# Hybrid GLA / RWKV-7 encoder block on one core: FFN rows, residuals and merged branches transposed by VectorE and through DRAM, and new operands used by two products at once

## The chip, the cores and the metric

The kernel runs on 1 core of a Trainium2 chip. Its time is the device time of one execution in microseconds (us). The time before is the median of 3 runs, and one more execution was profiled.

## The reference, cut to what matters

One layer of a streaming encoder on 256 frames of 2048 channels, all in float32. It has an FFN at half weight, a mixer with two branches, a second FFN at half weight and a final normalization.

```python
x = x + 0.5 * swiglu(rmsnorm(x, ffn1_norm), ffn1_wg, ffn1_wu, ffn1_wd)   # D_FF = 5632
h = rmsnorm(x, mix_norm)
p = h @ w_in                       # GLA heads | RWKV-7 heads (token shift) | two merge gates
o_gla = gla_branch(...)            # chunks of 64 frames, 4 heads
o_rw  = rwkv7_branch(...)          # delta-rule state, 16 heads of 64
gates = sigmoid(gate_p + gate_b)
merged = gates[..., :2048] * (o_gla @ w_branch[:1024]) + gates[..., 2048:] * (o_rw @ w_branch[1024:])
x = x + merged @ w_out
x = x + 0.5 * swiglu(rmsnorm(x, ffn2_norm), ffn2_wg, ffn2_wu, ffn2_wd)
out = rmsnorm(x, final_norm)

def swiglu(h, wg, wu, wd):
    return (silu(h @ wg) * (h @ wu)) @ wd
```

## The kernel before, in words

**Products.** Frames lie on 128 partitions, in NT = 2 row tiles. A product of activations and weights takes the activations transposed (channels on partitions) as the operand that TensorE loads, and a piece of the weights, 128 channels by NB = 512 columns, as the operand that streams. Both are split into a high and a low float32r part, and each K slice of 128 channels takes three matmuls per row tile: high times high, high times low, low times high. They write a PSUM tile `pm`, 128 rows by 512 columns, of which there are four. `linear` makes one block of 512 columns for both row tiles, over nk K slices; a block of 16 K slices is 96 matmuls.

**Weights.** `wload` issues on SyncE's queue one load of 1 MB for four K slices (`raw`, three buffers). For each half of it, a weight tile of two K slices, ScalarE casts it to `hi` (line 225) and VectorE subtracts that from `raw` to give `lo` (line 226). `hi` and `lo` have three buffers each. So a weight tile is one cast, one subtraction, and 12 matmuls, and the cast of a tile waits for the matmuls of the tile three before it.

**Who sets the order.** TensorE's instructions stay in the order in which the program is written (`mm`, `tr`). ScalarE's, VectorE's and the queues' are ordered when the kernel is built by a scheduler with a timeline of its own; weight casts and subtractions have a higher priority there. Work beside the products is written as generators: `later` puts one on a list with a due time, and `linear` calls `tick` after each K slice, which steps those that are due by a clock that counts 1.28 per K slice of full width. A `yield n` puts the next step off by n. An operand that isn't there yet is asked for through a function (`of`, `Normed.__call__`), which calls `drain` until it is. On each engine instructions run in order, and one that waits holds up those behind it.

**FFN.** D_FF is 11 blocks of 512 columns, taken in groups of 4, 4 and 3. For each block `linear` makes `pg` (with wg) and `pu` (with wu), 192 matmuls together. ScalarE writes silu(pg) into `h` and VectorE multiplies it with `pu`, one row tile at a time (lines 371 and 372). The generator `hidden` then brings the two row tiles of `h` into the layout with channels on partitions: `transposed` makes four TensorE transposes (128x128, line 117) into one PSUM tile `ps` per row tile, a set, and `split` casts that (ScalarE, line 288) and subtracts (VectorE, line 289) into the halves of `hid`. The down projection of the group is four `linear`s over 16 or 12 K slices of `hid`, and VectorE adds each to the residual x (line 392).

**Normalization.** `Normed` holds the transposed residual `xh`, `xl`, scaled by the norm's gain. The row scale 1/rms comes later, at the evacuation of each product. For each block of 512 channels `block` makes two sets of four TensorE transposes and, per K slice, a ScalarE activation (line 324) and a VectorE scalar_tensor_tensor (line 325); `stats` squares and sums on ScalarE (line 306). The first normalization reads the input, the second the residual after FFN 1, the third the residual after the mixer.

**Mixer.** The first product after the second normalization is the low-rank one (464 columns), then GLA's keys and query. The recurrence of RWKV-7 runs beside the products of the mixer; there VectorE already makes 32x32 block transposes (line 846), and POOL issues small loads (`uv`, `wg`) and writes gates to DRAM and reads them back (`md`). At the end `merge(j)` makes a block of 512 merged columns in `sg` and `mg`, and `split_up` transposes it as in the FFN. Four `linear`s over 16 K slices of these give the output projection; the residual is read back from DRAM into x2.

Of the kernel before, what the change touches and what calls it, by code (L numbers as in the profile page):

```python
# [71 lines left out]
def block_kernel(ctx, tc, A, out, dbg=None):  # L72
# [214 lines left out]
    def split(hi, lo, src):  # L287
        nc.scalar.copy(hi, src)
        nc.vector.tensor_sub(lo, src, hi.bitcast(F32))

    class Normed:
# [3 lines left out]
        def __init__(self, x, g0, first=False):  # L295
            self.x, self.g0, self.done, self.first = x, g0, 0, first
# [16 lines left out]

        def block(self, c):
            x, xh, xl = self.x, self.xh, self.xl
            for kt in range(4 * c, 4 * c + 4, 2):
# [10 lines left out]
                if kt == 0 and self.first:  # L327
                    warm_up(2)
# [3 lines left out]
        def __call__(self, kt, t):  # L332
            drain(lambda: self.done > kt // 2 / 2)
# [20 lines left out]
    def ffn(pool, x, xT, wg, wu, wd, then, by_rows=None):  # L354


        for b0, nb in ((0, 4), (4, 4), (8, 3)):
            hid = []

            def hidden(hs):  # L360
                hi, lo = mk(pool, [P, 4, SEQ], "hid", F32R, 12), mk(pool, [P, 4, SEQ], "hid", F32R, 12)
                yield from transposed(hs, hi, lo)
                hid.append((hi, lo))

            for b in range(b0, b0 + nb):
                pg = linear(xT, 16, cols(wg, b * NB))
                pu = linear(xT, 16, cols(wu, b * NB))
# [8 lines left out]
            for c in range(D // NB):  # L376
                w = cols(wd[b0 * NB:(b0 + nb) * NB], c * NB)
# [11 lines left out]
                pd = linear(xhl, 4 * nb, w)  # L389
# [7 lines left out]
    with phase("f1") as f1:  # L397
# [13 lines left out]
        n1 = Normed(x, R_F1, True)  # L411
# [4 lines left out]
        def to_mixer(c):  # L416
            if not n2:
                n2.append(Normed(x, R_MIX))
            later(n2[0].block(c), 1.5)
# [17 lines left out]
        lora_ps = linear(xT, 16, lora_cols, 464)  # L437
# [163 lines left out]
    later(gla_keys(rowscaled(linear(xT, 16, cols(w_in, K_OFF)))))  # L601
    later(chan_major([gq], rowscaled(linear(xT, 16, cols(w_in, Q_OFF))), 128 ** -0.5))
# [373 lines left out]
    mt = mixer.enter_context(phase("mt"))  # L976
    merged = []

    def merge(j, ps):
# [17 lines left out]
        later(split_up(), 1.5)  # L997
# [3 lines left out]
    xp = ctx.enter_context(tc.tile_pool(name="xp", bufs=1, side="right", reuse_waits="tile"))  # L1001
# [3 lines left out]
    n3 = None  # L1005
    for c in range(D // NB):
        ps = linear(xm, 16, cols(A["w_out"][0], c * NB))
# [3 lines left out]
        n3 = n3 or Normed(x, R_F2)  # L1011
        later(n3.block(c), 1.5)
# [45 lines left out]
```

## Time and profile before

| | |
|---|---|
| time | 2326.47 us, median of 3 runs (2326.31 to 2327.11) |
| the profiled execution | 2327.71 us, of it 2325.9 us span |
| TensorE busy | 2294.5 us, 99% |
| VectorE busy | 1283.8 us, 55% |
| ScalarE busy | 1025.8 us, 44% |
| POOL busy | 68.9 us, 3% |
| TensorE clock granted | 0.992 of full in the mean |
| SyncE's DMA queue (weights) | 52.9% of 16 engines' span |
| all DMA | 423.91 MB, mean 182 GB/s |

The span runs from the first to the last instruction of the profile. A busy share is the share of the span in which the engine ran at least one instruction; matmuls are pipelined, so TensorE's says little of its pace. Weight loads of TensorE run beside its matmuls and are counted apart. Idle time of an engine is put down to what ended it. The chain of waits is followed back from the last instruction, at each step to what released it.

### The profile page before, as it was taken

What the parts mean: (1) busy time and instruction counts of PE and PEld (TensorE: products, weight loads), DVE (VectorE), ACT (ScalarE), POOL (GpSimd) and SP (SyncE); (2) the same over time, 40 slices, a digit from 0 to 9 for tenths busy, and PEclk for the clock granted to TensorE, in tenths of its full rate; (3) what the DMA queues carried; (4) which work ended last, traced back from release to release, by engine and by line L of the source; (5) the groups of instructions that cost most, each with busy time, mean ns of one, the idle gap of its engine ahead of it and who ended that gap; (6) DMA issues with size and microseconds to landing.
All of it is one profiled execution on the core that took longest, in us unless ns stands there. A gap on an engine that the chain in (4) does not pass through costs nothing.

```text
span 2325.9 us, 29306 instructions
## 1 busy us (share of the span) xinstructions
PE 2294.5 (99%) x12123; PEld 1880.6 (81%) x12123; DVE 1283.8 (55%) x1435; ACT 1025.8 (44%) x1218; POOL 68.9 (3%) x119
## 2 busy tenths in 40 slices
PE   9999999999999999999999999999999999999998
PEld 7888888888888887877778778888888888888886
DVE  5445544554555545576677746655545544554555
ACT  5443344434445554454344334454443344434443
POOL 1000000000000001010101100000000000000000
PEclk9999999999999999999999999999999999999999
DMA  7555555556556554554334436656565656555553
GB/s 253 191 183 198 191 189 191 189 193 195 198 181 204 190 181 138 189 181 132 124 127 153 128 129 240 217 185 194 182 194 186 199 184 197 185 195 191 189 187 139
DMA packets 213157, 423.91 MB, mean 182 GB/s; under 512 B 10562, under 2 KB 14896, under 8 KB 212640
## 3 DMA queue, kind: packets, MB, share of 16 engines
q1 hardware_dynamic: 207072, 404.12, 52.9%
q0 software_dynamic: 5488, 17.12, 2.2%
q8 instruction: 95, 1.56, 0.3%
q10 hardware_dynamic: 464, 0.79, 0.1%
q14 instruction: 38, 0.31, 0.0%
HBM read 412.57 MB, written 7.34 MB: 181 GB/s over the span
## 4 chain that ended last, share of the span: by engine, by line
PE 94%; DVE 2%; ACT 2%; issue 1%; DMA 1%; POOL 0%; SPq 0%; DVEq 0%; ACTq 0%; POOLq 0%
PE pm L114 87%; PE ps L114 5%; PE ps L117 2%; DVE lo L226 1%; ACT hi L225 0%; DVE rn L710 0%; POOL uv L762 0%; DMA uv<-rv 0%; ACT L711 0%; DMA raw<-in_ffn_wd_dram 0%; DVE bk L752 0%; ACT L708 0%; DMA raw<-in_ffn_wg_dram 0%; ACT pt L704 0%; ACT at L706 0%
## 5 line engine op out<-in xcount | busy, mean ns | idle before, releaser
L226 DVE TENSOR_TENSOR lo<-raw,hi 128x1024 fp32r<-128x1024 f32 (+2 forms) x763 | 926.1, 1214 | 957.5 <-ACT hi L225 956.8
L225 ACT CAST hi<-raw 128x1024 fp32r<-128x1024 f32 (+2 forms) x763 | 796.8, 1045 | 1141.4 <-PE pm L114 1123.9
L114 PE MATMUL pm<-hi,xh 128*128 128x512 f32 (+1 forms) x2080 | 827.9, 398 | 0.3 <-ACT xh L324 0.3
L114 PE MATMUL pm<-lo,xh 128*128 128x512 f32 (+1 forms) x2080 | 813.6, 391 | 4.6 <-DVE lo L226 4.6
L114 PE MATMUL pm<-hi,xl 128*128 128x512 f32 (+1 forms) x2080 | 813.0, 391 | 0.0
L114 PEld LDWEIGHTS pm<-hi,xh 128*128 128x128 f32 x2080 | 392.6, 189 | 89.7 <-issue 7.7
L114 PEld LDWEIGHTS pm<-lo,xh 128*128 128x128 f32 x2080 | 393.0, 189 | 82.5 <-DVE lo L226 5.5
L114 PEld LDWEIGHTS pm<-hi,xl 128*128 128x128 f32 x2080 | 392.4, 189 | 82.7
L114 PE MATMUL pm<-hi,hid 128*128 128x512 f32 x1384 | 432.2, 391 | 0.0
L114 PEld LDWEIGHTS pm<-hi,hid 128*128 128x128 f32 x1384 | 259.9, 188 | 53.5
L114 PE MATMUL pm<-lo,hid 128*128 128x512 f32 x692 | 269.6, 390 | 1.6 <-DVE lo L226 1.6
L114 PEld LDWEIGHTS pm<-lo,hid 128*128 128x128 f32 x692 | 130.0, 188 | 28.4 <-DVE lo L226 2.0
L114 PE MATMUL pm<-hi,ot 128*128 128x512 f32 x256 | 86.9, 407 | 0.0
L114 PE MATMUL pm<-hi,mt 128*128 128x512 f32 x256 | 81.2, 393 | 0.0
L114 PEld LDWEIGHTS pm<-hi,ot 128*128 128x128 f32 x256 | 49.2, 192 | 11.3 <-issue 0.3
L114 PEld LDWEIGHTS pm<-hi,mt 128*128 128x128 f32 x256 | 48.1, 188 | 9.8
L114 PE MATMUL pm<-lo,ot 128*128 128x512 f32 x128 | 51.0, 399 | 0.0
L114 PE MATMUL pm<-lo,mt 128*128 128x512 f32 x128 | 49.9, 389 | 0.0
L371 ACT ACTIVATE h<-pm,rinv 128x512 f32<-128x512 f32 x44 | 30.2, 686 | 19.9 <-PE pm L114 19.9
L117 PEld LDWEIGHTS ps<-cst,h 128*128 128x128 f32 (+2 forms) x234 | 29.1, 140 | 7.5
L117 PE MATMUL ps<-cst,h 128*128 128x128 f32 (+2 forms) x234 | 34.9, 272 | 0.0
L324 ACT ACTIVATE xh<-ps,vec 128x256 fp32r<-128x256 f32 x48 | 22.5, 471 | 23.3 <-DVE xl L325 15.9
(242 smaller groups left out, 1064.2 us busy)
## 6 DMA issues: line engine op xcount, KB each, us to landing
raw<-in_ffn_wu_dram SPq DMA_DIRECT2D x88, 1024.0 KB, 5.2
raw<-in_ffn_wd_dram SPq DMA_DIRECT2D x88, 1024.0 KB, 5.0
raw<-in_ffn_wg_dram SPq DMA_DIRECT2D x85, 1024.0 KB, 5.2
raw<-in_w_in_dram SPq DMA_DIRECT2D x80, 1024.0 KB, 5.1
raw<-in_w_branch_dram SPq DMA_DIRECT2D x16, 1024.0 KB, 5.0
raw<-in_w_out_dram SPq DMA_DIRECT2D x16, 1024.0 KB, 5.1
raw<-in_w_in_dram SPq DMA_DIRECT2D x4, 896.0 KB, 5.7
raw<-in_ffn_wg_dram SPq DMA_DIRECT2D x12, 256.0 KB, 4.2
```

The lines of the kernel that those rows point to most:

```text
L114: tc.keep_in_program_order(nc.tensor.matmul(*args, **kw))
L117: tc.keep_in_program_order(nc.tensor.transpose(*args))
L225: nc.scalar.copy(hi[:, k0:k1, 0:width], src)
L226: nc.vector.tensor_sub(lo[:, k0:k1, 0:width], src, hi.bitcast(F32)[:, k0:k1, 0:width])
L324: nc.scalar.activation(xh[:, kt + j, :], ps[:, j, :], AF.Copy, scale=g)
L371: nc.scalar.activation(s, pg[t], AF.Silu, scale=xT.rinv[:, t:t + 1])
```

## The change

Three things are changed.

First, `turn` takes the place of TensorE's transposes for the FFN rows (`turned` in `hidden`), for the residuals of the second and third normalization (`turned_block`) and for the merged branches (`split_up`). VectorE transposes each 128x512 row tile in 32x32 blocks into `blocks` (one buffer). A DMA that POOL issues writes `blocks` to DRAM (`aside`, 0.5 MB, two buffers), and four DMAs that POOL issues, one per group of 32 channels, read it back into `turned` (two buffers), which then holds channels on partitions. ScalarE's cast and VectorE's subtraction read `turned`, in SBUF, in the place of `ps`, in PSUM. The first normalization, GLA's outputs and the small transposes of the recurrence stay with TensorE.

Second, `two_linears` makes two products that use the same operand: the K slices of the first, all but the last group of four; then the same of the second; then the last group of the first, then of the second. It is used for the first gate and up block of each FFN, for the low-rank and key product, for the first two blocks of each down projection, and for the first two of the output projection.

Third, small things: the pool of x2 opens before the merge, since the merge now keeps its tiles there; the warm-up matmuls are tied to the first block of `block` alone; the query product is written ahead of the keys' evacuation.

```diff
+    def two_linears(xhl, nk, w0, w1, width0=NB):
+        last = nk // 4 - 1
+        pss = [linear(xhl, nk, w, n, kgs=range(last)) for w, n in ((w0, width0), (w1, NB))]
+        return [linear(xhl, nk, w, n, ps, [last]) for (w, n), ps in zip(((w0, width0), (w1, NB)), pss)]
...
+    def turn(pool, srcs):
+        blocks = mk(pool, [P, NT, 4, P], "blocks", F32, 1)
+        for t, src in enumerate(srcs):
+            nc.vector.transpose(blocks[:, t].rearrange("p b (k j) -> p b k j", k=4),
+                                src.rearrange("p (k b j) -> p b k j", k=4, b=4))
+        aside = dram.tile([P, NT, 4, P], F32, tag="aside", name=nm("aside"), bufs=2)
+        nc.gpsimd.dma_start(aside, blocks)
+        res = mk(pool, [P, NT * 4, 4, 32], "turned", F32, 2)
+        for b in range(4):
+            nc.gpsimd.dma_start(
+                res[32 * b:32 * b + 32].rearrange("i (t g) k j -> i t g (k j)", t=NT),
+                aside[:, :, b].rearrange("(g i) t n -> i t g n", g=4))
+        return res
...
+        def turned_block(self, c):
+            x, xh, xl = self.x, self.xh, self.xl
+            res = turn(self.pool, [x[:, t, c * NB:(c + 1) * NB] for t in range(NT)])
+            self.stats(c)
+            for k in range(4):
+                if k % 2 == 0:
+                    yield 1.0 if k else 4.0
+                kt = 4 * c + k
+                g = col(self.g0 + kt)
+                nc.scalar.activation(by32(xh[:, kt, :]), res[:, :, k, :], AF.Copy, scale=g)
+                nc.vector.scalar_tensor_tensor(
+                    by32(xl[:, kt, :]), res[:, :, k, :], g, by32(xh.bitcast(F32)[:, kt, :]), ALU.mult, ALU.subtract)
+                self.done += 0.25
...
+    def turned(pool, srcs, hi, lo):
+        res = turn(pool, srcs)
+        for t in range(NT):
+            yield 1.0 if t else 4.0
+            ts = slice(t * P, (t + 1) * P)
+            h4, l4 = (a[:, :, ts].rearrange("p k (g j) -> p k g j", j=32) for a in (hi, lo))
+            split(h4, l4, res[:, 4 * t:4 * t + 4].rearrange("p g k j -> p k g j"))
...
             def hidden(hs):
...
-                yield from transposed(hs, hi, lo)
+                yield from turned(pool, hs, hi, lo)
...
-                pg = linear(xT, 16, cols(wg, b * NB))
-                pu = linear(xT, 16, cols(wu, b * NB))
+                if b == 0:
+                    pg, pu = two_linears(xT, 16, cols(wg, 0), cols(wu, 0))
+                else:
+                    pg, pu = linear(xT, 16, cols(wg, b * NB)), linear(xT, 16, cols(wu, b * NB))
...
+            pds = two_linears(xhl, 4 * nb, *ws[0:2])
...
-                pd = linear(xhl, 4 * nb, w)
+                pd = pds[c] if c < 2 else linear(xhl, 4 * nb, w)
...
-            later(n2[0].block(c), 1.5)
+            later(n2[0].turned_block(c))
...
-        lora_ps = linear(xT, 16, lora_cols, 464)
+        lora_ps, key_ps = two_linears(xT, 16, lora_cols, cols(w_in, K_OFF), 464)
...
-            yield from transposed([s[:, t, :] for t in range(NT)], hi, lo)
+            yield from turned(xp, [s[:, t, :] for t in range(NT)], hi, lo)
...
+    pos = two_linears(xm, 16, *wos[0:2])
...
-        n3 = n3 or Normed(x, R_F2)
-        later(n3.block(c), 1.5)
+        n3 = n3 or Normed(x, R_F2, xp)
+        later(n3.turned_block(c))
```

The order of the instructions moves at the places where a transposed block is taken into the two halves. First ScalarE in the FFN, from the third weight tile before the end of the second block's products on. `hi` is a weight tile, made from `raw`; `hid` is the high half of the transposed block, made from the PSUM tile `ps`. Before:

```order
L225 CAST hi_841<-raw_839 128x1024
L225 CAST hi_845<-raw_839 128x1024
L225 CAST hi_891<-raw_889 128x1024
L225 CAST hi_895<-raw_889 128x1024
L288 CAST hid_855<-ps_863 128x4x128
L225 CAST hi_925<-raw_923 128x1024
L288 CAST hid_855<-ps_882 128x4x128
L225 CAST hi_929<-raw_923 128x1024
L225 CAST hi_959<-raw_957 128x1024
L225 CAST hi_963<-raw_957 128x1024
L225 CAST hi_995<-raw_993 128x1024
```

and after, with `turned` in the place of `ps`:

```order
L225 CAST hi_841<-raw_839 128x1024
L225 CAST hi_845<-raw_839 128x1024
L225 CAST hi_889<-raw_887 128x1024
L225 CAST hi_893<-raw_887 128x1024
L225 CAST hi_925<-raw_923 128x1024
L225 CAST hi_929<-raw_923 128x1024
L225 CAST hi_959<-raw_957 128x1024
L225 CAST hi_963<-raw_957 128x1024
L294 CAST hid_855<-turned_862 128x4x128 x2
L225 CAST hi_995<-raw_993 128x1024
```

The two casts of the block stood behind the second and the third weight tile of the next block (`raw_889`, `raw_923`); they now stand together behind three more tiles than the second of them did, ahead of the tile `hi_995`.

VectorE at the same place, from the last product of the rows on (`h`, line 372 before and 423 after). `lo` is the other half of a weight tile. Before:

```order
L372 SCALAR_TENSOR_TENSOR h_126_831<-pm_693,rinv_105,h_126_831 128x512
L372 SCALAR_TENSOR_TENSOR h_127_834<-pm_694,rinv_105,h_127_834 128x512
L226 TENSOR_TENSOR lo_892<-raw_889,hi_891 128x1024
L226 TENSOR_TENSOR lo_896<-raw_889,hi_895 128x1024
L289 TENSOR_TENSOR hid_856<-ps_863,hid_855 128x4x128
L226 TENSOR_TENSOR lo_926<-raw_923,hi_925 128x1024
L289 TENSOR_TENSOR hid_856<-ps_882,hid_855 128x4x128
```

and after, where `blocks` is the tile of 32x32 blocks that goes to DRAM:

```order
L423 SCALAR_TENSOR_TENSOR h_127_831<-pm_693,rinv_105,h_127_831 128x512
L423 SCALAR_TENSOR_TENSOR h_128_834<-pm_694,rinv_105,h_128_834 128x512
L303 STREAM_TRANSPOSE blocks_857<-h_127_831 128x512
L226 TENSOR_TENSOR lo_890<-raw_887,hi_889 128x1024
L303 STREAM_TRANSPOSE blocks_857<-h_128_834 128x512
L226 TENSOR_TENSOR lo_894<-raw_887,hi_893 128x1024
L226 TENSOR_TENSOR lo_926<-raw_923,hi_925 128x1024
L226 TENSOR_TENSOR lo_930<-raw_923,hi_929 128x1024
L226 TENSOR_TENSOR lo_960<-raw_957,hi_959 128x1024
L226 TENSOR_TENSOR lo_964<-raw_957,hi_963 128x1024
L295 TENSOR_TENSOR hid_856<-turned_862,hid_855 128x4x128 x2
```

Two block transposes have come in, with a weight subtraction between them, and the block's own subtractions stand behind six weight subtractions where they stood behind two and three.

Last ScalarE at the first residual block of the second normalization, in the down projection that ends FFN 1. Line 306 before and 332 after is the squaring for the row statistics; `xh` is the high half of the transposed residual. Before:

```order
L225 CAST hi_4825<-raw_4823 128x1024
L306 ACTIVATE h_788_4819,part_4761<-x_87 128x512
L306 ACTIVATE h_789_4821,part_4761<-x_87 128x512
L225 CAST hi_4829<-raw_4823 128x1024
L324 ACTIVATE xh_4763<-ps_4795,vec 128x256 x2
L225 CAST hi_4859<-raw_4857 128x1024
L324 ACTIVATE xh_4763<-ps_4810,vec 128x256 x2
```

and after:

```order
L225 CAST hi_4875<-raw_4873 128x1024
L332 ACTIVATE h_817_4899,part_4865<-x_87 128x512
L332 ACTIVATE h_818_4901,part_4865<-x_87 128x512
L225 CAST hi_4879<-raw_4873 128x1024
L225 CAST hi_4945<-raw_4943 128x1024
L332 ACTIVATE h_822_4913,part_4865<-x_87 128x512
L332 ACTIVATE h_823_4915,part_4865<-x_87 128x512
L225 CAST hi_4949<-raw_4943 128x1024
L225 CAST hi_4987<-raw_4985 128x1024
L349 ACTIVATE xh_4867<-turned_4894,vec 128x256 x4
L225 CAST hi_4991<-raw_4985 128x1024
```

The four activations of the block stand together behind later weight tiles. The squaring of the second residual block (`h_822`, `h_823`) now comes ahead of them, since `two_linears` ends the first two blocks of the down projection close together.

## Rows read from the trace of the kernel before

**Rows 1.** Page, busy us, share, instructions of each engine.

```profile
PE 2294.5 (99%) x12123; PEld 1880.6 (81%) x12123; DVE 1283.8 (55%) x1435; ACT 1025.8 (44%) x1218; POOL 68.9 (3%) x119
```

**Rows 2.** Page, chain of waits, share of the span by line.

```profile
PE pm L114 87%; PE ps L114 5%; PE ps L117 2%; DVE lo L226 1%; ACT hi L225 0%; DVE rn L710 0%; POOL uv L762 0%; DMA uv<-rv 0%; ACT L711 0%; DMA raw<-in_ffn_wd_dram 0%; DVE bk L752 0%; ACT L708 0%; DMA raw<-in_ffn_wg_dram 0%; ACT pt L704 0%; ACT at L706 0%
```

**Rows 3.** Chain from 100 to 400 us: start us, us, what.

```profile
106.53 40.84 PE pm L114 x180
147.37 0.44 PE ps L117 x4
147.81 2.76 PE pm L114 x12
...
151.00 40.84 PE pm L114 x180
...
195.47 127.88 PE pm L114 x564
```

**Rows 4.** TensorE transposes by form: busy us, mean ns, idle before.

```profile
L117 PE MATMUL ps<-cst,h 128*128 128x128 f32 x228 | 34.3, 272 | 0.0
...
L117 PE MATMUL ps<-cst,x 128*128 128x128 f32 x96 | 15.3, 285 | 0.0
...
L117 PE MATMUL ps<-cst,sg 128*128 128x128 f32 x16 | 2.4, 272 | 0.0
...
L117 PE MATMUL ps<-cst,mg 128*128 128x128 f32 x16 | 2.4, 272 | 0.0
```

**Rows 5.** ScalarE by form, same columns, idle with what ended it.

```profile
L225 ACT CAST hi<-raw 128x1024 fp32r<-128x1024 f32 x743 | 782.0, 1053 | 1129.0 <-PE pm L114 1115.2 <-issue 12.7 <-DMA raw<-in_ffn_wg_dram 0.9
...
L288 ACT CAST hid<-ps 128x512 fp32r<-128x512 f32 x44 | 25.5, 579 | 0.0
...
L324 ACT ACTIVATE xh<-ps,vec 128x256 fp32r<-128x256 f32 x48 | 22.5, 471 | 23.3 <-DVE xl L325 15.9 <-PE ps L117 7.4
```

**Rows 6.** VectorE by form, same columns.

```profile
L226 DVE TENSOR_TENSOR lo<-raw,hi 128x1024 fp32r<-128x1024 f32 x743 | 909.2, 1224 | 946.6 <-ACT hi L225 946.0
...
L846 DVE STREAM_TRANSPOSE xt<-xx 128x512 f32<-128x512 f32 x16 | 11.3, 708 | 0.3
```

**Rows 7.** Windows, FFN 1 and mixer: busy us (instructions), granted clock, DMA share.

```profile
106.00:670.00 564.00, 564.00 (x2523) 467.20 (x2522) 280.22 (x253) 235.58 (x240) 0.61 (x1) 1.00 0.58 191
749.00:909.00 160.00, 159.48 (x698) 122.96 (x696) 81.83 (x93) 78.48 (x98) 0.00 (x0) 1.00 0.53 177
```

**Rows 8.** Timeline from 188 us: start, us, operation, [idle <-releaser].

```profile
188.66 1.41 DVE L372 SCALAR_TENSOR_TENSOR h<-pm,rinv,h 128x512 f32<-128x512 f32 x2
189.15 1.06 ACT L225 CAST hi<-raw 128x1024 fp32r<-128x1024 f32 x1 [1.67 <-PE pm L114]
190.23 1.23 DVE L226 TENSOR_TENSOR lo<-raw,hi 128x1024 fp32r<-128x1024 f32 x1 [0.17 <-ACT hi L225]
```

**Rows 9.** Tiles md, wg, uv: issue ns, stretch; us to landing.

```profile
L964 POOL DMA_DIRECT2D md<-mg x4: 552/566/597, 1156.2 to 1323.4; - x4
...
DMA to landing us min/median/max: 3.0/4.4/6.9
...
L737 POOL DMA_DIRECT2D wg<-in_rwkv_w_g_dram x4: 722/734/747, 923.1 to 1349.8; - x4
...
DMA to landing us min/median/max: 3.3/4.7/6.4
...
DMA to landing us min/median/max: 1.8/2.9/5.7
```

**Rows 10.** Timelines of VectorE and of POOL about 1349 us.

```profile
1349.50 0.71 DVE L846 STREAM_TRANSPOSE xt<-xx 128x512 f32<-128x512 f32 x1
...
1349.79 0.75 POOL L737 DMA_DIRECT2D wg<-in_rwkv_w_g_dram  x1 [11.27 <-PE ps L114]
```

**Rows 11.** Timeline of VectorE about 726 us.

```profile
725.86 1.28 DVE L392 SCALAR_TENSOR_TENSOR x<-pm,x 128x512 f32<-128x512 f32 x2
```

**Rows 12.** Page, loads of wg: KB each, median us to landing.

```profile
raw<-in_ffn_wg_dram SPq DMA_DIRECT2D x85, 1024.0 KB, 5.2
```

More of the change, by code (lines that the diff above doesn't have):

```diff
@@ L289, in split, with by32, __init__ @@
         nc.vector.tensor_sub(lo, src, hi.bitcast(F32))
+    def turn(pool, srcs):
[11 more added lines that the diff above has]
+        return res
+    def by32(a):
+        return a.rearrange("p (u j) -> p u j", j=32)
     class Normed:
-        def __init__(self, x, g0, first=False):
-            self.x, self.g0, self.done, self.first = x, g0, 0, first
+        def __init__(self, x, g0, pool=None):
+            self.x, self.g0, self.done, self.pool = x, g0, 0, pool
             self.part = tn([P, NT, 4], "part")
@@ L326, in block @@
                         xl[:, kt + j, :], ps[:, j, :], g, xh.bitcast(F32)[:, kt + j, :], ALU.mult, ALU.subtract)
-                if kt == 0 and self.first:
+                if kt == 0:
                     warm_up(2)
@@ L332, in __call__ @@
         def __call__(self, kt, t):
-            drain(lambda: self.done > kt // 2 / 2)
+            drain(lambda: self.done > kt / 4)
             return self.xh[:, kt, t * P:(t + 1) * P], self.xl[:, kt, t * P:(t + 1) * P]
@@ L375, in ffn @@
             xhl = of(hid)
-            for c in range(D // NB):
-                w = cols(wd[b0 * NB:(b0 + nb) * NB], c * NB)
+            ws = [cols(wd[b0 * NB:(b0 + nb) * NB], c * NB) for c in range(D // NB)]
+            pds = two_linears(xhl, 4 * nb, *ws[0:2])
+            for c, w in enumerate(ws):
                 if by_rows and b0 == 8 and c == 3:
@@ L410, in block_kernel @@
         later(vectors(mk(f1, [P, P], "rows")))
-        n1 = Normed(x, R_F1, True)
+        n1 = Normed(x, R_F1)
         for c in range(4):
@@ L417, in to_mixer @@
             if not n2:
-                n2.append(Normed(x, R_MIX))
-            later(n2[0].block(c), 1.5)
+                n2.append(Normed(x, R_MIX, f1))
+            later(n2[0].turned_block(c))
         ffn(f1, x, n1, A["ffn1_wg"][0], A["ffn1_wu"][0], A["ffn1_wd"][0], to_mixer)
@@ L599, in gla_out @@
         tap("gla_T0", oglaT[0][0].bitcast(F32))
-    later(gla_keys(rowscaled(linear(xT, 16, cols(w_in, K_OFF)))))
-    later(chan_major([gq], rowscaled(linear(xT, 16, cols(w_in, Q_OFF))), 128 ** -0.5))
+    query_ps = linear(xT, 16, cols(w_in, Q_OFF))
+    later(gla_keys(rowscaled(key_ps)))
+    later(chan_major([gq], rowscaled(query_ps), 128 ** -0.5))
     for res, off, func in ((gv, V_OFF, AF.Copy), (gr, R_OFF, AF.Silu)):
@@ L976, in block_kernel @@
     mt = mixer.enter_context(phase("mt"))
+    xp = ctx.enter_context(tc.tile_pool(name="xp", bufs=1, side="right", reuse_waits="tile"))
     merged = []
@@ L993, in split_up @@
             hi, lo = mk(mt, [P, 4, SEQ], "mt", F32R, 8), mk(mt, [P, 4, SEQ], "mt", F32R, 8)
-            yield from transposed([s[:, t, :] for t in range(NT)], hi, lo)
+            yield from turned(xp, [s[:, t, :] for t in range(NT)], hi, lo)
             merged.append((hi, lo))
-        later(split_up(), 1.5)
+        later(split_up())
     for j in range(4):
         merge(j, started[j] if j < 2 else None)
-    xp = ctx.enter_context(tc.tile_pool(name="xp", bufs=1, side="right", reuse_waits="tile"))
     x = mk(xp, [P, NT, D], "x2")
@@ L1005, in block_kernel @@
     n3 = None
+    wos = [cols(A["w_out"][0], c * NB) for c in range(D // NB)]
+    pos = two_linears(xm, 16, *wos[0:2])
     for c in range(D // NB):
-        ps = linear(xm, 16, cols(A["w_out"][0], c * NB))
+        ps = pos[c] if c < 2 else linear(xm, 16, wos[c])
         for t in range(NT):
```

## The prediction

> **What bounds the kernel now.** I read the busy table first. TensorE is busy in 99% of the span [rows 1]. A busy share alone doesn't prove that the engine works at its full pace, so I read the chain of waits next: 87% of the span is the products that write pm, 5% the small products of GLA and the recurrence, 2% the TensorE transposes of line 117, 1% the subtraction that ends a weight tile [rows 2]. The reader is to see there that TensorE's own instruction list sets the end nearly alone. The groups by line say the same from the other side: ScalarE's weight casts were idle 1129.0 us and 1115.2 us of that ended with a product of pm, which freed their buffer [rows 5]. ScalarE and VectorE wait for TensorE, not the reverse. In the FFN stretch VectorE is busy 280.22 of 564 us and the DMA engines 0.58 of the time [rows 7], so both have room.
>
> So an instruction that leaves TensorE's list shortens the run by what it held TensorE, as long as nothing else becomes late.
>
> **What the change removes.** Count the sets of four transposes that go. FFN rows: 11 blocks in each of two FFNs, two sets per block, 44 sets (176 of the 228 instructions that read h [rows 4]). Residuals: the second and third normalization, four blocks of two sets each, 16 sets (64 of the 96 that read x; the first normalization keeps its own). Merged branches: four blocks of two sets, 8 sets (all of those that read sg and mg [rows 4]). Together 68 sets, 272 instructions. The products stay 9120, and the same in kind.
>
> What one set costs is read from the chain, not from the 272 ns of a single transpose, which overlap [rows 4]. From 106.53 to 151.00 us one FFN block passes, 192 products and two sets [rows 3]: 44.47 us. A long stretch without a transpose gives the pace of a product: 127.88 us over 564 is 0.2267 us [rows 3]. 192 of them are 43.53 us, so two sets cost 0.94 us, one 0.47 us (the piece shows 0.44, and the product behind it starts a little late). 68 sets at 0.47 us are 31.8 us.
>
> **What it adds, and what lies beside what.** Each of the 34 turns adds on VectorE two block transposes of 128x512; the same operation took 708 ns in the recurrence [rows 6], so 68 of them are 48 us more on an engine that is about half idle. They read 128-byte runs with a stride there, which no row shows; between equal time and double, 0.71 and 1.4 us each, I take 0.71, the row's. The casts and subtractions stay in number and size: two casts of 579 ns per FFN block [rows 5], now read from SBUF instead of PSUM. And each turn adds five POOL DMAs through DRAM, 0.5 MB out and 0.5 MB back: some 34 MB beside 424 MB, with DMA engines busy 0.58 [rows 7].
>
> The price that matters is latency, because engines work in order. In an FFN block the first cast that reads the turned data stands behind the casts of eight weight tiles (a tile: one cast, two K slices, 12 products, 2.72 us), counted from the last product of the block; before, the two casts that read PSUM stood two and three tiles earlier. While that cast waits for the DMA, the next weight cast waits behind it on ScalarE, and the subtraction behind it on VectorE; TensorE waits for both. So there is a latest landing. Let T0 be the block's last product. There are three weight buffers, so tile 7 (counted from 0) is cast when tile 4 is used up, at T0 + 13.6 us, and is done at 14.7. Tile 8 may be cast from T0 + 16.3 on, and TensorE needs it at T0 + 21.8. Cast and subtraction together take 2.31 us (cast at 189.15, subtraction over at 190.23 + 1.23 [rows 8]), so ScalarE has to begin tile 8 by T0 + 19.4, and the two turned casts before it by T0 + 18.2.
>
> When does the turn land? VectorE begins the gating product 0.1 us after T0 and takes 1.41 us for two rows [rows 8], then a transpose (0.71), a weight subtraction that the order puts between (1.23), a transpose (0.71): T0 + 4.2. The write to DRAM is like md's, 0.5 MB from a POOL issue: 4.4 us median, 3.0 to 6.9 [rows 9]; landed at T0 + 8.6. Then POOL issues four reads one after another, 0.75 us each as for wg [rows 10], so the fourth starts at T0 + 10.9. A read of 128 KB in 512-byte pieces has no row. From below the 32 KB transfers of uv, 1.8 us at best; from above the slowest of wg's 256 KB transfers, 6.4 [rows 9]. I take wg's median, 4.7, the nearest in shape. T0 + 15.6, with 2.6 us to spare; the ends are T0 + 11.3 (3.0 and 1.8) and T0 + 19.8 (6.9 and 6.4), the latter 1.6 us too late. I cost the 22 FFN turns at nothing; their cover is ScalarE's gap before tile 8 and the two weight tiles that are cast ahead.
>
> The residual blocks are tighter. The first and third block of the second normalization and the first of the third have their four casts of 471 ns [rows 5] behind seven tiles, not eight: latest start T + 13.6 + 3.1 - 1.9 = T + 14.8. The sum there is 0.1 + 1.28 (the residual add, two rows [rows 11]) + 1.42 + 4.4 + 2.3 + 4.7 = T + 14.2. At three places 0.6 us to spare: I put 0.5 us at each for landings later than the median, 1.5 us in all; by the ends, from nothing to 3 x 3.6 = 11 us. The other blocks, and all four merged ones, have two more tiles or more.
>
> The products that would need the newest block at once (the first two of a down projection, the low-rank and key projections, the first two of the output projection) now run all other K blocks of both first: six K blocks of 5.44 us, 33 us after T0 (22 us where there are three blocks), against some 17 us for turn and casts. So there no product waits for a turn; weights, loads and POOL's other work stay as many. The low-rank and key results are evacuated later and closer together; from 749 to 909 us TensorE idled 0.52 of 160 us in all [rows 7], and I leave it at nothing, between 0 and 1 us. In the recurrence the instruction lists of TensorE, ScalarE and VectorE are the same as before; nothing there moves.
>
> **Sum.** The profiled execution took 2327.71 us, 2325.9 of it span, 1.24 us above the median 2326.47. 2327.71 - 31.8 + 1.5 = 2297.4 for it; 2296 for the median.
>
> **The rivals.**
> Slower: the turn lands too late. One mechanism, at ScalarE's turned cast in the 22 FFN blocks: each microsecond past T0 + 18.2 is a microsecond of TensorE idle, since tile 8 can't be cast. It turns the gain over from 30.3 / 22 = 1.4 us late on average, a landing at T0 + 19.6. At the upper end, T0 + 19.8 and the three residual places at 3.6 us, the time is 2294.7 + 22 x 1.6 + 11 = 2341. For it: the read back is not in the trace, and four of them share the DMA engines with a 1 MB weight load (5.2 us to landing [rows 12]). Against it: it takes the slowest write and the slowest read in every block.
>
> Partly late: some blocks hit a weight load and lose 1 us in half of the FFN turns, 11 us, and 1 us more at each of the three tight places, 3 us: 2296 + 14 = 2310. For it speaks the spread of landings [rows 9], against it the 2.6 us.
>
> POOL's issues are held by VectorE. If each of the five issues of a turn waited for a VectorE instruction of 0.71 to 1.22 us, a landing would come 3.5 to 6.1 us later, T0 + 19.1 to 21.7, and the 22 blocks lose 0.9 to 3.5 us each: 2315 to 2372. Against it: a wg issue at 1349.79 ran 0.75 us while a block transpose of VectorE had begun at 1349.50 [rows 10], no longer than one needs without. This is a rule of the Trainium skill (SBUF — State Buffer, Who interferes with whom): a VectorE instruction in a mode that takes both ports shuts GpSimd out, and with it the writing of DMA descriptors. The row bears out only that neither the block transpose nor the subtraction is such a one here.
>
> No gain, because the weights set the pace: if casts or loads were the bound, TensorE would just idle where the transposes were, 2326. Against it the 1115.2 us that the casts waited for TensorE [rows 5].
>
> **How the numbers follow.** Forecast 0.74; partly late 0.12; landing too late 0.06; POOL held 0.03; no gain 0.04; something not seen 0.01. The forecast's own range is 2293 to 2302: below, no loss at all and a set at 0.48 us; above, the tight residual places at half their bound. To hold 8 in 10 it has to take in the partly late case: 2293 to 2314. What a measurement of this kernel can tell from no change is about 0.2%, 4.7 us. Faster 0.87, same 0.05 (no gain and part of the mixed cases), slower 0.08.
>
> **What would show it.** Right: one FFN block takes 43.5 us instead of 44.47 in the chain; line 117 keeps 52 transposes that read h and 32 that read x, none that reads sg or mg; TensorE stays at 99% with no product waiting for a turned cast; ScalarE's turned cast waits little or nothing for its DMA. Wrong: products of pm wait for ScalarE's or VectorE's weight tiles once per FFN block, with the turned cast ended by a DMA just before; or turned's median to landing above 7 us; or POOL issues of over 1 us each.

## The result, and the profile after

The changed kernel took 2301.1 us, the median of 4 runs (2297.67 to 2302.71), where the kernel before took 2326.39 us in the runs beside it: a ratio of 0.989, with an interval of 0.9873 to 0.9907. The forecast was 2296 us. Run again later beside other kernels it took 2298.76 us against 2324.82 us, 0.9882 (0.9868 to 0.9897). So some 25 to 26 us are gained of the 30 forecast. The profiled executions took 2327.71 us before, a little more than any of the four runs, and 2302.71 us after, the slowest of its four; their spans, 2325.9 and 2300.9 us, differ by 25.0 us.

Busy time, share of the span and number of instructions by engine, after:

```profile
span 2300.9 us, 29227 instructions
PE 2263.7 (98%) x11851; PEld 1851.5 (80%) x11851; DVE 1319.1 (57%) x1503; ACT 1026.2 (45%) x1218; POOL 171.6 (7%) x289
```

TensorE has 272 instructions fewer and VectorE 68 more than in [rows 1], but TensorE is idle for 37.2 us of the span (span less busy time) where it was for 31.4: there is idle time now that was not there. Next the groups by line of the kernel after (busy us, mean ns of one, idle time before them and what ended it), against [rows 4 to 6]:

```profile
L117 PE MATMUL ps<-cst,h 128*128 128x128 f32 x52 | 7.6, 272 | 0.0
...
L117 PE MATMUL ps<-cst,x 128*128 128x128 f32 x32 | 5.3, 293 | 0.0
...
L303 DVE STREAM_TRANSPOSE blocks<-h 128x512 f32<-128x512 f32 x44 | 30.7, 699 | 0.0
...
L294 ACT CAST hid<-turned 128x512 fp32r<-128x512 f32 x44 | 25.0, 618 | 3.5 <-DMA turned<-aside 3.5
...
L349 ACT ACTIVATE xh<-turned,vec 128x256 fp32r<-128x256 f32 x32 | 13.7, 498 | 9.1 <-DMA turned<-aside 9.1
...
L294 ACT CAST mt<-turned 128x512 fp32r<-128x512 f32 x8 | 4.6, 617 | 11.1 <-DMA turned<-aside 11.1
```

Of the transposes 52 read h and 32 read x, none sg or mg. A block transpose took 699 ns, where one in the recurrence had taken 708 [rows 6]. The last column tells the rest: 44 casts of FFN rows waited 3.5 us for their DMA in all, 32 of residuals 9.1 us, and the 8 of merged branches 11.1 us.

The same product stands at the same number in both kernels, so its start can be compared. The lead of the changed kernel, worked out from the two traces:

| the product at | before, us | after, us | lead, us |
|---|---|---|---|
| start of the mixer | 749.19 | 735.11 | 14.1 |
| start of the merge | 1447.79 | 1432.90 | 14.9 |
| just before the first merged cast | 1486.77 | 1469.62 | 17.1 |
| first product of the output projection | 1494.16 | 1482.58 | 11.6 |
| its product 120 | 1523.13 | 1511.48 | 11.7 |
| second block of FFN 2 | 1632.51 | 1617.56 | 14.9 |
| last down projection | 2254.44 | 2229.56 | 24.9 |

The lead grows by 0.945 us at each of the 22 FFN blocks and at each of the eight residual blocks. Within the mixer it goes up and down, between 12.0 us (product 4416) and 18.1 us (product 3484), and ends 0.8 us higher than it began. That is not the change alone: between the two profiles of the changed kernel the mixer up to the merge differs by 0.9 us as well. Behind the mixer the lead falls at one place, the merge, though sets were removed there too. There TensorE waited (timeline, TensorE, after):

```profile
1472.20 0.50 PE L114 MATMUL pm<-hi,ot 128*128 128x512 f32 x1 [1.05 <-ACT hi L225]
1474.33 0.80 PE L114 MATMUL pm<-lo,ot 128*128 128x512 f32 x1 [1.63 <-DVE lo L226]
1474.93 1.05 PE L114 MATMUL pm<-hi,ot 128*128 128x512 f32 x2
1475.78 0.63 PE L114 MATMUL pm<-lo,ot 128*128 128x512 f32 x1
```

and ScalarE, at the same time, held a weight cast behind the first merged branch's casts:

```profile
1470.06 1.14 ACT L294 CAST mt<-turned 128x512 fp32r<-128x512 f32 x2 [5.98 <-DMA turned<-aside]
1471.11 2.93 ACT L225 CAST hi<-raw 128x1024 fp32r<-128x1024 f32 x3
```

The turned cast waited 5.98 us for its DMA, three weight casts followed at once, and TensorE idled 1.05 and 1.63 us. The products behind the waits come every 0.43 us where they came every 0.227. That is the granted clock (windows of the kernel after: us, busy time of TensorE, its weight loads, VectorE, ScalarE, POOL with their instructions, granted clock, DMA share, GB/s):

```profile
1456.00:1468.00 12.00, 12.00 (x54) 9.95 (x53) 8.51 (x10) 3.17 (x3) 3.55 (x6) 1.00 1.00 318
1470.00:1474.00 4.00, 1.65 (x7) 0.79 (x5) 3.29 (x4) 3.94 (x5) 0.90 (x2) 0.96 0.73 283
1474.00:1480.00 6.00, 5.67 (x13) 4.46 (x14) 3.73 (x5) 0.61 (x2) 2.15 (x4) 0.50 0.76 223
1480.00:1486.00 6.00, 6.00 (x27) 4.89 (x26) 5.49 (x7) 3.08 (x5) 2.41 (x4) 0.95 0.96 272
```

From 1474 to 1480 us TensorE was granted 0.50, its lower level of 1.2 GHz: 13 recorded products where 6 us hold 26. The lead fell by 5.6 us there, and one set that was removed in this stretch hid 0.5 more: 6.0 us, 2.7 of it idle and most of the rest slow products. A second, smaller stop (0.24 and 0.76 us idle about 1508 us, at the fourth branch) cost 1.7 us in the same way of counting. Together 7.7 us.

The first row also points to a cause: the DMA engines are busy 1.00 of 1456 to 1468 us. Before, in the same place of the program:

```profile
1471.00:1483.00 12.00, 12.00 (x60) 9.96 (x59) 9.19 (x11) 5.66 (x8) 0.53 (x1) 1.00 0.60 216
```

The 2 MB read that brings the residual back, which the change could have moved into this stretch, isn't in it: it landed at 1424.6 us. The landings tell of the crowding too. The tile views of `turned`, after, first from 40 to 700 us (FFN 1 and the first residual blocks), then in the merge:

```profile
L309 POOL DMA_DIRECT2D turned<-aside x47: 599/631/677, 62.3 to 699.5; - x47
DMA to landing us min/median/max: 4.1/4.8/6.0
```

```profile
L309 POOL DMA_DIRECT2D turned<-aside x16: 599/643/679, 1460.3 to 1498.1; - x16
DMA to landing us min/median/max: 2.7/7.3/8.1
```

4.8 us in the median there, 7.3 here. The issues take 0.63 and 0.64 us in both.

### The profile page after: what moved, and what is told of

The parts are those of the page before. It is cut to its first block, busy times and chain, and to the rows that moved or that the text cites. A ratio compares the mean times of both kernels' runs of the same rounds, so it can differ in the third digit from the quotient of the medians.

```text
span 2300.9 us, 29227 instructions
## 1 busy us (share of the span) xinstructions
PE 2263.7 (98%) x11851; PEld 1851.5 (80%) x11851; DVE 1319.1 (57%) x1503; ACT 1026.2 (45%) x1218; POOL 171.6 (7%) x289
## 5 line engine op out<-in xcount | busy, mean ns | idle before, releaser
L226 DVE TENSOR_TENSOR lo<-raw,hi 128x1024 fp32r<-128x1024 f32 (+1 forms) x763 | 924.1, 1213 | 890.5 <-ACT hi L225 889.8
L225 ACT CAST hi<-raw 128x1024 fp32r<-128x1024 f32 (+1 forms) x763 | 796.2, 1045 | 1117.4 <-PE pm L114 1095.0
L114 PE MATMUL pm<-hi,hid 128*128 128x512 f32 x1384 | 427.2, 389 | 0.0
L306 POOL DMA_DIRECT2D aside<-blocks x34 | 19.8, 581 | 1256.8 <-DVE blocks L303 1254.9
L309 POOL DMA_DIRECT2D turned<-aside x136 | 82.4, 635 | 131.0 <-DMA aside<-blocks 90.6
L114 PEld LDWEIGHTS pm<-hi,ot 128*128 128x128 f32 x256 | 50.0, 195 | 13.1 <-ACT hi L225 1.5
L114 PEld LDWEIGHTS ps<-xx,ak 64*64 64x64 f32 x640 | 21.0, 139 | 13.7 <-DVE xx L896 7.9
```

The costliest lines, as they stand in the source:

```text
L114: tc.keep_in_program_order(nc.tensor.matmul(*args, **kw))
L225: nc.scalar.copy(hi[:, k0:k1, 0:width], src)
L226: nc.vector.tensor_sub(lo[:, k0:k1, 0:width], src, hi.bitcast(F32)[:, k0:k1, 0:width])
L306: nc.gpsimd.dma_start(aside, blocks)
L309: nc.gpsimd.dma_start(res[32 * b:32 * b + 32].rearrange("i (t g) k j -> i t g (k j)", t=NT), aside[:, :, b].rearrange("(g i) t n -> i t g ...
```

## The experiments

All are compared with the kernel before, run on the same chip beside them. They were run in three sets, in which the kernel before took 2324.8, 2325.7 and 2326.1 us, so a difference between rows of two sets is good to about 1 us. The differences between the first six rows are smaller than their intervals; their traces tell them apart.

| kernel | median, us | ratio to before (interval) |
|---|---|---|
| changed kernel, again | 2298.76 | 0.9882 (0.9868 to 0.9897) |
| merged branches by TensorE | 2297.85 | 0.9884 (0.9867 to 0.9900) |
| merged casts pinned later | 2298.16 | 0.9881 (0.9866 to 0.9895) |
| no read of the GLA part | 2298.68 | 0.9883 (0.9868 to 0.9898) |
| first and fourth by TensorE | 2296.92 | 0.9882 (0.9866 to 0.9899) |
| first alone by TensorE | 2298.83 | 0.9889 (0.9872 to 0.9907) |
| casts behind 6 tiles | 2331.84 | 1.0024 (1.0011 to 1.0037) |
| turns 4 us later | 2326.62 | 1.0003 (0.9988 to 1.0018) |
| casts behind 4 tiles | 2475.61 | 1.0648 (1.0626 to 1.0669) |
| products in the old order | 2317.95 | 0.9970 (0.9957 to 0.9983) |
| two at once, no turn | 2326.03 | 1.0001 (0.9991 to 1.0010) |

Whole spans don't separate the first six either. Their program is the same in the mixer up to the merge, and still this stretch took up to 2.2 us less in their profiles than in the first one of the changed kernel. So the merge is measured by itself: what the lead over the kernel before fell short of the removed sets, 0.4725 us each, from the start of the merge to product 5680, behind the fourth branch (worked out from the traces; the 7.7 us above are the two stops alone):

| kernel | lost in the merge, us |
|---|---|
| changed kernel, first profile | 7.8 |
| changed kernel, again | 4.3 |
| merged branches by TensorE | 0.0 |
| merged casts pinned later | 2.7 |
| no read of the GLA part | 5.9 |
| first and fourth by TensorE | 0.5 |
| first alone by TensorE | 2.1 |

**The changed kernel, again.** 

> The changed kernel as it is, run again beside the others. 2301 us, with single runs from 2297 to 2303 as before. In its profile the products stop for 5.2 us at the first merged branch and 1.2 us at the fourth, or for less in a run that is nearer to 2297: the theory that the cost sits there says that the spread of its runs comes from there too.

Its waits at the first merged branch were 0.44 and 1.62 us, none at the fourth, and its profiled run took 2298.4 us. The product after the two places starts 4.3 us earlier than in the first profile, 0.7 us of which it had won before them. So 3.6 of the 4.3 us between the two profiles come from there. That the spread of all runs does is not shown by two profiles.

**Merged branches by TensorE.** `turned(xp, ...)` in `split_up` becomes `transposed(...)` again. 

> Only the four merged branches go back to TensorE's transposes (8 sets, 0.475 us each, 3.8 us). Theory A (all that the change fell short of its forecast is lost at the merged branches, 6.4 us): 2301.1 - 6.4 + 3.8 = 2298.5 us, and single runs closer together. Theory B (the loss is spread over the kernel, so that the merged branches gain like the rest): 2301.1 + 3.8 = 2305 us.

Theory A in the trace: no wait of a product between 1400 and 2200 us, the granted clock 1.00 in the whole stretch from 1440 to 1530 us (0.96 in the first profile of the changed kernel), the DMA engines busy 0.65 of 1456 to 1468 us where they were busy 1.00, and nothing lost in the merge. From the start of the merge to its end this kernel gains 4.1 us on the changed one, though 8 sets are back, 3.8 us: together the 7.7 us. (The 6.4 us of the expectation was an earlier count.) In time it is within 1 us of the changed kernel run beside it: what turning the merged branches took off TensorE's list and what it cost are about equal.

**Merged casts pinned later.** The casts and subtractions of the four branches are kept in program order, with due times of 21.5, 21.5, 16.3 and 26.6 in the place of 4. By the trace they then stand behind 10, 10, 9 and 12 weight tiles. 

> The merged branches are turned as in the changed kernel, but ScalarE's casts of the first and fourth stand behind 10 and 14 weight tiles instead of 8 and 9; the same DMAs. Theory A1 (the loss is ScalarE's cast standing in front of weight casts while its data are on the way): the first may now land 23.6 us after its last product where it landed at 21.1, so both losses go: 2301.1 - 6.4 = 2294.7 us, weight loads still 8 to 10 us to landing there. Theory A2 (the DMA engines are overfull there and weight loads of 8 to 10 us are themselves late): no more than 2 us come back, 2299 to 2301 us, with casts of hi waiting for raw.

A1 holds for ScalarE: the first merged cast now waits 0.56 us and holds nothing up. But TensorE waits 1.59 us all the same, a little later, and VectorE shows why (timeline of TensorE, then of VectorE):

```profile
1474.70 0.50 PE L114 MATMUL pm<-lo,ot 128*128 128x512 f32 x1 [1.59 <-DVE lo L226]
```

```profile
1472.23 1.30 DVE L306 STREAM_TRANSPOSE blocks<-sg 128x512 f32<-128x512 f32 x2 [4.29 <-DMA aside<-blocks]
1473.46 1.18 DVE L226 TENSOR_TENSOR lo<-raw,hi 128x1024 fp32r<-128x1024 f32 x1
```

The third branch's block transposes need `blocks`, of which there is one, and the second branch's write out of it takes 10.3 us to land. The weight subtraction stands behind. It is neither theory as written: one wait is gone, and the next one in the same crowded stretch has taken its place. The profile lost 2.7 us in the merge, less than either profile of the changed kernel; its time isn't told apart from theirs.

**No read of the GLA part.** `mr` is loaded for the first two branches only and used again. 

> The third and fourth merged branch do not read their GLA part back from DRAM but add that of the first and second (part of the computation is changed); 1 MB of reads leaves the stretch in which the first two turns are under way, one of them just ahead of the first turn's write on POOL's queue. If crowding by these reads makes the first turn late: its write takes 3 to 4.4 us instead of 5.5 and its reads 5 to 6.5 instead of 7.9, so 2 to 3.5 us of the 5.2 come back, 2297.5 to 2299 us. If the weight loads alone crowd it: 2301 us.

Inconclusive. Without the reads of `mr` the four reads of the first turn took 6.0 us in the median where they had taken 7.8, as expected, so these reads are a part of the crowding. But in the order that resulted POOL waited for one more VectorE instruction and issued the write 1.8 us later, and the write took 5.5 us as before: the turn landed at 20.8 us after the evacuation where it had landed at 21.0, and the stop was as long.

**First and fourth by TensorE.** 

> The first and the fourth merged branch are transposed by TensorE (4 sets, 1.9 us), the second and third turned. If the first turn is late because two turns and the weight loads share the DMA engines in that stretch, no product waits there now: 7.7 us of loss in the first profile of the changed kernel go and 1.9 come back, 2295 to 2297 us, and 1.9 us less than with all four by TensorE. If each merged turn is late by itself (the addition of the GLA part makes it start later), the second and third lose 2 us or more each: 2299 us or more.

No product waits in the merge, and against the kernel with all four by TensorE it goes from 0.3 us behind to 1.5 us ahead between 1457 and 1474 us, where the second and third branch's four sets were. Some 0.3 us of that is lost again at the first transpose of the fourth branch. So the second and third turn stop no product when the other two are gone. The windows, against the same stretches above:

```profile
1456.00:1468.00 12.00, 12.00 (x57) 9.99 (x56) 9.82 (x11) 4.81 (x5) 3.51 (x6) 1.00 0.91 305
...
1474.00:1480.00 6.00, 6.00 (x27) 4.75 (x26) 4.97 (x7) 4.15 (x6) 2.42 (x4) 1.00 0.92 271
```

TensorE runs through at the full clock beside DMA engines that are still busy 0.91 and 0.92. The median is the lowest of all kernels run, 2296.92 us, but not by more than the interval.

**First alone by TensorE.** 

> The first merged branch alone is transposed by TensorE (2 sets, 0.95 us). If its turn overlapping with the second one's is what made it late: the first stop is gone, the fourth branch's 1.2 us may stay, 2295 to 2298 us. If each merged turn is late by itself: a stop at the second, 2299 us or more.

Its time, 2298.83 us, lies between the two expectations; the trace decides. The first stop is gone, and there is none at the second and third. The fourth waits, as in the first profile:

```profile
1497.88 0.50 PE L114 MATMUL pm<-hi,mt 128*128 128x512 f32 x1 [0.82 <-ACT hi L225]
1499.14 0.50 PE L114 MATMUL pm<-lo,mt 128*128 128x512 f32 x1 [0.76 <-DVE lo L226]
```

With the first turn gone the second lands 18.6 us after its evacuation, where it landed at 23.0: two turns one behind the other delay each other. In the new order its cast stands behind eight tiles, so 18.6 is just at the limit found below. The fourth, behind eight tiles too, lands at 19.6 and is late without such a neighbour; from its first read to the last landing it took 10.4 us beside the weight loads of the output projection. So the crowding by a second turn isn't the whole cause.

**Casts behind 6 tiles.** In `turned` of the FFN the due time is 11.2 and the casts are kept in program order, the next weight cast behind them:

```diff
-            yield 1.0 if t else 4.0
+            yield 1.0 if t else wait or 4.0
...
+        if pinned:
+            tc.keep_in_program_order(a)
+            tc.keep_in_program_order(b)
+            behind[0] = True
```

> In the 22 FFN blocks ScalarE's casts and VectorE's subtractions of the turned rows stand behind 6 weight tiles instead of 8; the same instructions and DMAs. Theory of the latest landing (each us after the limit is a us of TensorE): the limit moves from 18.2 to 12.8 us after the block's last product, landings are at 13.4 to 17.3 us (sum of what is over: 39 us), so 2301 + 39 = 2340 us, 2333 to 2347. Rival (ScalarE and VectorE have enough room to catch up, the order of their work costs nothing): 2301 us.

Measured 33 us above the changed kernel, where 39 were expected; 31 us of it are in the 22 FFN blocks of the profile. The rival falls.

**Turns 4 us later.** 

> POOL does two more small operations (2.2 us each) between the landing of the write and the issue of the reads in the 22 FFN turns, with the casts behind 8 weight tiles as in the changed kernel. By the limit of 18.2 us and the landings of the profile, moved by 4.3 us, 16 us are lost (9 to 26 with the limit 0.5 us later or earlier): 2317 us, 2310 to 2327. If the cover was larger than the 2.6 us of the prediction: 2301 us.

The time lies inside the range, near its upper end, but it is 28 us above the changed kernel as run again, where 16 were expected; 23 us are in the 22 blocks of the profile. The reads were issued 4.8 us later than in the changed kernel, not 4.3.

**Casts behind 4 tiles.** As with 6, with a due time of 6.1. 

> As tiles_6, with the casts of the 22 FFN turns behind 4 weight tiles. By the runs so far a turn loses what its landing is behind the limit (18.5 us after the block's last product with 8 tiles, 13.1 with 6), so the limit is 7.6 us here, each turn about 6.8 us late: 22 x 6.8 = 150 us, 2299 + 150 = 2449 us, if a wait costs its length alone. If each such wait is followed by products at half the granted clock, as those behind the waits of 3 us in tiles_6 and the first merged branch were (2.7 us lost there besides the wait): 22 x 9.5 = 209 us, 2508 us, and the granted clock of the whole run below 0.98.

177 us above the changed kernel, in the 22 blocks of the profile 8.05 us each: between the two expectations. One of the stops (timeline of TensorE, then windows with the clock):

```profile
118.09 0.39 PE L114 MATMUL pm<-hi,xl 128*128 128x512 f32 x1
123.22 0.80 PE L114 MATMUL pm<-hi,xh 128*128 128x512 f32 x1 [4.74 <-ACT hi L227]
124.48 0.79 PE L114 MATMUL pm<-lo,xh 128*128 128x512 f32 x1 [0.46 <-DVE lo L228]
125.07 0.63 PE L114 MATMUL pm<-hi,xl 128*128 128x512 f32 x1
```

```profile
124.00:130.00 6.00, 5.54 (x16) 4.38 (x16) 2.69 (x3) 1.68 (x3) 0.00 (x0) 0.58 0.55 168
130.00:132.00 2.00, 2.00 (x11) 1.65 (x10) 1.23 (x1) 0.44 (x1) 0.00 (x0) 1.00 0.06 22
```

From the three kernels, what a turn that landed late cost (both worked out from the traces: landing from the start of the evacuation, loss from the start of the same product in the changed kernel):

| casts behind | landing, us | lost, us |
|---|---|---|
| 8 tiles | 13.4 to 17.3 (22 turns of the changed kernel) | 0 |
| 8 tiles | 19.14 / 20.78 / 21.63 / 22.20 (four of the 22 turns 4 us later) | 0.50 / 2.17 / 2.91 / 6.37 |
| 6 tiles | 13.69 / 14.61 / 14.92 / 15.51 / 17.68 (five of 22 turns) | 0.58 / 1.42 / 1.73 / 3.92 / 6.78 |
| 4 tiles | 13.4 to 15.1 (22 turns) | 7.4 to 8.8 |

While the clock stays up, the loss is what the landing is behind a limit: 18.6 us with 8 tiles, 13.1 with 6. Where TensorE then runs on at 0.50 of its clock the loss jumps by 1.5 to 2.8 us more: 15.51 lost 3.92 where the line gives 2.4, and 22.20 lost 6.37 where it gives 3.6 (granted clock 0.57 over the 8 us behind it). Not every such wait did it: 21.63 lost 2.91, on the line, at a clock of 1.00. In the kernel with 4 tiles each turn was some 6.2 us late by the same line (limit 7.7 us, an estimate from the other two), and lost 1.9 us more than that on average.

**Products in the old order.** The FFNs' `two_linears` become `linear`s one after another. 

> The FFNs' products one after another again, without two at once (first gate and up block, first two of each down projection); the turns stay. If the interleaving is what hides the newest block: the down projection of a group of three blocks asks for it 10.9 us after its last product, it is ready at about 16.4, so 5.5 us are lost in each FFN; a group of four asks at 16.3 us, 0 to 1 us lost each; with up to 2 us at the first block of FFN 2: 11 to 17 us, about 2315 us. If the two-at-once order is worth nothing: 2301 us.

19 us above the changed kernel, where 11 to 17 were expected on top of 2301 us. The two groups of three blocks lost 6.9 and 6.3 us, as in this row at the second one, which half-clock products follow; the four groups of four lost 0 to 1 us each, and the first block of FFN 2 about 2.6:

```profile
2247.28 0.79 PE L114 MATMUL pm<-hi,hid 128*128 128x512 f32 x1 [3.27 <-ACT hid L294]
```

**Two at once, no turn.** The kernel before with `two_linears` alone. 

> The kernel before with the two-at-once order alone, all transposes by TensorE. If that order only makes room for a late operand: no change, 2326 us within 2. If the products waited for new operands in the kernel before: some us faster.

No change, as expected: the order gains nothing by itself, and in the FFNs it is worth 19 us once operands come late. What it is worth at the mixer's first products and at the output projection wasn't tried.

## Why the prediction was right, point by point

**What bounds the kernel, and what a set costs: right.** The lead grows by 0.945 us per FFN block, 0.4725 us a set, where the sum had 0.47. A long piece of the chain after has no transpose in it, at 200.37 / 884 = 0.2267 us a product as in [rows 3], so 192 products take 43.5 us:

```profile
1599.82 200.37 PE pm L114 x884
```

68 sets at that rate are 32.1 us, 31.8 forecast.

**The FFN turns at nothing: right, with the right cover.** Landings came 13.4 to 15.6 us after the evacuation's start in 21 of 22 turns and once at 17.3 us, against the T0 + 15.6 of the sum, whose T0 is 0.1 us earlier. The write was quicker than md's (3.1 us in the median of all 34, not 4.4) and the read as chosen from wg (4.8 us, not 4.7). The limit, forecast at T0 + 18.2, was measured at T0 + 18.5 by the delayed turns and at T0 + 13.0 with two tiles fewer; the two tiles are 5.5 us, and twice the 2.72 us of the forecast is 5.4. At the fourth block's casts ScalarE has no wait for the DMA (timeline, after):

```profile
200.48 1.14 ACT L294 CAST hid<-turned 128x512 fp32r<-128x512 f32 x2
202.25 1.06 ACT L225 CAST hi<-raw 128x1024 fp32r<-128x1024 f32 x1 [0.63 <-PE pm L114]
```

**The three tight residual places: 1.5 us forecast, nothing lost.** Their landings, 13.5 and 15.6 us in the second normalization and 14.0 in the third, were near the 14.2 of the sum; one was behind the limit of 14.8 and still stopped no product, so that limit was set too tight: the measured 18.5 less one tile of 2.72 us is 15.8 (an estimate). The upper bound of the forecast's range, 2302 us, adds half of the 11 us of these places to a sum that already has 1.5 us for them; by its own terms it is 2300 us, below the first median of 2301.1. The casts of all residual blocks waited 9.1 us.

**The newest block hidden by two products at once: right.** Without that order 19 us are lost in the FFNs.

**The low-rank and key products at nothing, and a mixer that doesn't move: not quite.** Against the kernel with the order alone, the changed one lost 1.1 us around these products, in three holds of 0.3 to 0.4 us (products 3181, 3193 and 3301), at the upper end of the 0 to 1 us of the forecast. It isn't the order, which both have; what held the products stays open. In the recurrence the order is the same, but its length is not fixed: profiles of kernels that are the same there differ by 1 to 2 us, and here that went the other way by 1.5 us.

**The merged branches at nothing: wrong.** This is the step that failed: "The other blocks, and all four merged ones, have two more tiles or more." More than the seven of the tight places, that is nine. By the order of ScalarE's casts the first merged branch stands behind eight, the fourth behind nine, and the second and third behind ten, so the count was wrong for the first alone, and eight were enough in the FFN. The larger error is the landing, which isn't the FFN's. The GLA part is added first, so the first write is issued 5.6 us after the evacuation's start, not 4.0. Two turns follow each other within 6 us, the DMA engines are busy 1.00 of 12 us, the write takes 5.5 us and the reads 7.8. The first landed at 21.0 us, the other three at 23.1 to 24.5. By the measured limit of 18.6 us with eight tiles and 2.72 us for one more, the first was 2.4 us late and the fourth 1.8 (an estimate). I had taken DMA room from a window of the FFN [rows 7] for a stage that has less time between its turns. The cost in the first profile was 7.7 us; 32.1 - 7.7 = 24.4, and with the 0.7 us by which the lead at the start of the merge, 14.9, is above the 30 sets removed until there, 14.2, that is 25.1, against 25.0 between the spans. No set was removed for these 0.7 us; they are what the start and the mixer leave over, and partly chance. That the median still came within some 5 us of the forecast is because the error sits at four turns of 34, of which only two stopped TensorE.

**The size of a late landing: too small.** The rival of a late landing took each us late as a us of TensorE. That holds for the smaller delays; where the clock falls, its price comes on top. At the merge the stop cost 6.0 us, with 2.7 us idle.

**POOL's issues held by VectorE: fell.** 136 issues of reads took 0.64 us in the median, 34 of writes 0.58, 0.68 at most, beside an engine busy 57% of the time. The row of the forecast [rows 10] shows this for the block transpose alone, since no subtraction ran beside that issue. In the trace after, 106 of the 170 issues ran beside a weight subtraction and nine beside a block transpose, the longest 0.68 us, and so was the longest of the 57 that had no instruction of VectorE beside them for more than 0.1 us. The rule of the Trainium skill (SBUF — State Buffer, Who interferes with whom) stands untouched: no run here had a VectorE instruction that shut POOL out.

On the crowding, the Trainium skill (DMA: Bandwidth & Descriptors, Queues, rings and completion order) says that a DMA engine takes turns between the queues that have work for it. The trace agrees as far as it goes: while the second branch's write was under way for 9.6 us, the weight loads of SyncE's queue took 8.9 and 9.4 us, where their median in the mixer is 5.1. Both slow down.

**What stays open.** The gain forecast for a version without the stops, some 2 us below the changed kernel, isn't resolved by the times of any of the variants. What the turned first branch waited for most, its own write and reads or the weight loads between them, wasn't separated. That the crowding makes the turns late is shown as far as the stretch goes with fewer turns: the fewer were turned there, the shorter the stops. Which transfer costs which is open.

## What to carry to other kernels

An engine that sets the end is relieved by what leaves its list, at the price of one item in a long piece of the chain, provided that the replacement lands before the in-order engines that feed it reach the instruction that waits. Work out that latest landing per place, by counting the weight tiles in the order ahead of the waiting cast, and take the DMA's time from a stretch as busy as the one it will run in. A new operand that comes late is best covered by products that don't need it: the order that did it here gained nothing alone and, in the FFNs, 19 us with the turn.

## What the runs showed that was not expected

A wait of TensorE can cost more than its length. After waits of 1.05 and 1.63 us with one product between them the granted clock was 0.50 for some 6 us, and the whole stop cost 6.0 us; after 4.74 and 0.46 us (casts behind 4 tiles) it was 0.58 in the mean of the next 6 us and 1.00 again in the two behind. Most turns that came late cost their lateness alone, though, with the clock at 1.00. So a gap in a stretch of products without any can be dearer than it looks, and the granted clock behind it tells whether it was.
